# A split-fp32 FFN on one core: a product put off, the last two units reordered, the hidden output stored as ready-made blocks

## The chip, the cores and the metric

The kernel runs on one core of one Trainium2 chip. The metric is the device time of one execution in microseconds (us), lower is better. Engines are named as in the profile: PE (TensorE), DVE (VectorE), ACT (ScalarE), POOL (GpSimd), SP (the queue that issues the DMAs).

## What is computed

Four layers on x of 1024 tokens by 1024 features in float32: two hybrid layers, then two layers of retention and differential attention, each of which ends in an FFN. Only that FFN is touched:

```
u = rmsnorm_2(h, ffn_norm[l])
h = h + (jax.nn.silu(u @ w_gate[l]) * (u @ w_up[l])) @ w_down[l]   # hidden width 2816
```

## The kernel before

**Arithmetic.** A float32 product is made of three matmuls in a rounded format: high by high, high by low, low by high. So each operand is first split: ACT rounds it to `hi` (for weights L1268, L204, L1516; for activations L1202), and another engine subtracts, `lo = src - hi` (weights on POOL, L193 and L1517; activations on POOL or DVE, L1203). `block` (L1187 to 1196) issues the three matmuls for each 128-row chunk of the contraction (L1192, L1194, L1195).

**Seven products.** Both FFN products are cut 2 by 2 and made from seven block products in place of eight. The activations then stand as the blocks B11, B21, B22 and the differences T1 to T4; the weights get four DVE operations a unit (`combine`, L1321 to 1324 and L1500 to 1503), in place, so that w6, w3 take the place of the first row's two blocks and w7, w4 that of the second's.

**First half, `ffn_hidden` (L1272 to 1388).** 22 units: unit i makes 256 columns of the gate (i even) or the up projection (i odd) for all tokens; two units make a pair j. `first` runs two block products (24 matmuls), `second` the other five (60). Each of the four quadrants of a unit's result goes to `leave`. For the gate it is scaled by the row factor R (DVE, L230), ACT takes a tanh (L1285), DVE combines (L1286), and POOL multiplies by R again (L1287). For the up projection DVE multiplies it into the gate's z (L1281). After an odd unit the pair's two chunks of z go to DRAM (L1351). The FFN's normalized input lives as blocks in nine `xp` buffers and five in `fx`.

**Second half, `ffn_out` (L1461 to 1591).** The hidden chunks are taken in five groups of four (NSG) and two left over (`dense_ops`). A group has four units, one for each pair of output chunks, of 7 block products by 2 chunks by 3 matmuls, 42 in all. Seven DVE additions a unit take the products out of PSUM into the residual (L1561 to 1582); several of them must be done before PE may go on accumulating in the same bank. `hidden_blocks` (L1390) prepares the next group meanwhile: a list of steps, of which `some()` takes one at four places of each unit. A group's steps are: eight loads of 256 KB (L1401), eight DVE subtractions that make T1 to T4 (`minus`, L1417), and 14 splits (L1202, L1203). For group 0 the loads and the first steps stand in the last turn of the first half's loop, the rest ahead of the second half's first unit. A unit's weights are split in seven pieces of 256 columns (L1516, L1517).

**Order.** The program is built with `schedule_with_timeline_sim=True`: the order on each engine is set by a simulated timeline, so instructions that are independent do not run in the order in which they are written; `issue_after` adds an edge of order on one engine. A tile is a buffer of a pool (`xp` has 13, `wp` three for each of whi and wlo); whoever wants one that is in use waits until its last reader is done.

Of the kernel before, what the change touches and what calls it, by code (L numbers as in the profile page):

```python
# [24 lines left out]
P = 128  # L25
# [12 lines left out]
FDENSE = NH - 4 * NSG  # L38
LEAD, SW = 4, 2
IB, IT = 1, 2  # L40
EPS = 1e-6
# [31 lines left out]
class Builder:  # L73
    def __init__(self, nc, tc, a, es):
        self.nc, self.tc, self.a, self.es = nc, tc, a, es
        self.n = 0
        self.pools = {}
        self.chains = []
        self.ready, self.use_ready = [], False
        self.open(es, cp=1, rp=1, wp=3, xp=13, dp=6, sp=8)  # L80
        self.open(es, bass.MemoryType.PSUM, pa=3, ps=2, pt=2, po=1)
        self.open(es, bass.MemoryType.DRAM, dr=2)
# [1024 lines left out]
    def second(self, l, last):  # L1107
# [3 lines left out]
        with contextlib.ExitStack() as es:  # L1111
# [32 lines left out]
            self.open(es, fx=6, sw=SW, p1=LEAD)  # L1144
# [127 lines left out]
    def ffn_hidden(self, wg, wu, X, scale, more):  # L1272

        nc = self.nc
        Z, sums, hd = {}, {}, []

        def leave(i, u, t, src):
# [20 lines left out]
        def first(i, r, hold=False):  # L1298
            w = (wg, wu)[i % 2][i // 2 * 2]
            part = lambda j: (self.load_w(w[:, 4 * j:4 * j + 4, :]) if r is None else  # L1300
                              self.wsplit(r[:, 0, j * HW:(j + 1) * HW]))
# [25 lines left out]
        def second(i, w5, w3, w6, w7, w4):  # L1327
            s = sums.pop(i)
            C, E, B = self.psT(), self.psO(), self.psS()
            p5, w, u2, u3 = (self.d2() for _ in range(4))  # L1330
            self.block(C, self.wsplit(w5), X["T1"], True)
            nc.scalar.copy(p5, C)
            self.block(E, self.wsplit(w3), X["B22"], True)
            tt(w, E, p5, ALU.add)
            self.block(B, self.wsplit(w6), X["T2"], True)
            tt(u2, B, s, ALU.add)
            tt(w, w, u2, ALU.add)
            leave(i, 0, t1, w)
            self.block(B, self.wsplit(w7), X["T3"], False)
# [4 lines left out]
            self.block(C, self.wsplit(w4), X["T4"], True)  # L1344
            tt(u3, u3, C, ALU.subtract)
            leave(i, 1, t0, u3)
            if i % 2:
                z = Z.pop(i // 2)
                for u in range(2):
                    h = self.tl("dr", (P, S), tag="h", bufs=NH)  # L1350
                    nc.sync.dma_start(h, z[:, u, :])  # L1351
                    hd.append(h)

# [21 lines left out]
        for i in range(NH):  # L1375
            if i > 1:
                r = raw(i)
                if i == NH - 1:
                    ahead = self.hidden_blocks(hd, 0)
                    ahead[1].pop(0)()  # L1380
                if i >= LEAD:
                    first(i, r)
                ws.append(combine(r))
            if i == NH - 1:
                for _ in range(NAH):
                    ahead[1].pop(0)()
            second(i, *ws[i])
        return hd, ahead

    def hidden_blocks(self, hd, g):  # L1390
# [5 lines left out]
        def load(k):  # L1396
            two = self.tl("xp", (P, 4, HW))
            for h in range(2):
                for u in range(2):
                    f[u, h, k] = two[:, 2 * u + h, :]  # L1400
                    nc.sync.dma_start(f[u, h, k], hd[4 * g + 2 * u + k][:, h * HW:(h + 1) * HW])  # L1401

        def loads():
            for k in range(2):
                load(k)

        def put(name, k, slot, h, src, eng, sub=None):
            def step():
                if sub is not None:
                    sub()  # L1410
                if slot not in q:
                    q[slot] = self.tl("hx" if g % 2 else "xp", (P, 2, S), F32R)
                self.put_block(X, name, k, q[slot], h, f[src], eng)
            steps.append(step)

        def minus(eng, o, x, y):
            return lambda: eng.tensor_tensor(f[o], f[x], f[y], ALU.subtract)  # L1417

        for k in range(2):
            b11, b12, b21, b22 = (0, 0, k), (0, 1, k), (1, 0, k), (1, 1, k)  # L1420
            put("B11", k, k, 0, b11, v)
        for k in range(2):
            b11, b12, b21, b22 = (0, 0, k), (0, 1, k), (1, 0, k), (1, 1, k)
            put("T1", k, 2 + k, 0, b11, v, minus(v, b11, b12, b11))
        for k in range(2):
            put("B21", k, k, 1, (1, 0, k), p)
        for k in range(2):
            b11, b12, b21, b22 = (0, 0, k), (0, 1, k), (1, 0, k), (1, 1, k)
            put("B22", k, 2 + k, 1, b22, p, minus(v, b12, b22, b12))
            put("T2", k, 4 + k, 0, b22, v, minus(v, b22, b22, b11))  # L1430
        for k in range(2):
            b11, b12, b21, b22 = (0, 0, k), (0, 1, k), (1, 0, k), (1, 1, k)
            put("T3", k, 4 + k, 1, b12, p)
            put("T4", k, 6, k, b21, p, minus(v, b21, b21, b22))
        return X, [loads] + steps

    def dense_ops(self, wd, hd, c0):
# [5 lines left out]
        def load():  # L1443
            for c in range(c0, NH):
                o = self.tl("hx", (P, 2, S), F32R)
                f = self.tl("xp", (P, S))
                nc.sync.dma_start(f, hd[c])
# [30 lines left out]
    def ffn_out(self, l, hd, last, ahead):  # L1478
# [27 lines left out]
        parts, pmark = [], [None]  # L1506

        def wsplit(src):

            if not parts:  # L1510
                hi = self.tl("wp", (P, 4, P), F32R, tag="whi")
                lo = self.tl("wp", (P, 4, P), F32R, tag="wlo")
                parts.extend([(hi[:, 0:2, :], lo[:, 0:2, :]), (hi[:, 2:4, :], lo[:, 2:4, :])])
            hi, lo = parts.pop(0)
# [3 lines left out]
            return hi, lo  # L1518

        def weights(r):  # L1520
            w1, w2 = wsplit(r[0][:, 0:n]), wsplit(r[0][:, n:2 * n])
            return w1, w2, combine(r)
# [16 lines left out]
        X, steps = ahead  # L1539
        for f in steps:  # L1540
            f()
        residual(0)
        rs = raw(1)
        for i in range(4 * NSG):
# [12 lines left out]
            w1, w2, (w5, w3, w6, w7, w4) = ready  # L1557
# [4 lines left out]
            self.block(C, wsplit(w5), X["T1"], True)  # L1562
# [4 lines left out]
            self.block(A, wsplit(w6), X["T2"], False)  # L1567
# [4 lines left out]
            self.block(C, wsplit(w3), X["B22"], False)  # L1572
# [5 lines left out]
            w4 = wsplit(w4)  # L1578
# [159 lines left out]
def layout(i):  # L1738
# [22 lines left out]
    a["w_down_2"] = units(i["w_down_2"], KC)  # L1761
# [26 lines left out]
```

## Time and profile before

| | |
|---|---|
| three runs, median (lowest to highest) | 3586.26 us (3582.91 to 3586.89) |
| profiled execution, own time | 3588.15 us |
| its span, mean granted TensorE clock | 3586.4 us, 0.977 |
| first half of the FFN, steady part | 1660 to 2025 us, and 2905 to 3295 us in the other layer |
| from the first to the second half | 2025 to 2105 us, 3295 to 3365 us |
| second half, steady part | 2105 to 2290 us, 3365 to 3540 us |

A row of the windows view tells, for a stretch of the span, how long each engine was busy in it and with how many instructions, the clock that TensorE was granted, the share of the time in which the DMA engines were busy, and the rate. A row of the waits view tells who waited for whose result: us in total, how often, the longest. A wait in PE's column is time in which the array stands; idle time of another engine costs nothing by itself.

### The profile page before, as it was taken

The numbers are of one execution on the slowest core, as the hardware profiler recorded it, in microseconds if no ns is written. First come the engines' busy times: TensorE is split into PE (matmuls) and PEld (weight loads), VectorE is DVE, ScalarE is ACT, GpSimd is POOL, SyncE is SP. The second block draws the span as 40 slices with busy tenths as digits, with TensorE's granted clock in tenths as the row PEclk, the third lists the DMA queues.
The fourth block names the chain that finished last, engine by engine and source line by source line (L and its number), as shares of the span: only waits on it lengthen the run. The fifth ranks groups of instructions, "written<-read, shape, count | busy, mean of one in ns | idle before, by whom it ended". The sixth has DMA issues, their size and how long they took to land.

```text
span 3586.4 us, 46309 instructions
## 1 busy us (share of the span) xinstructions
PE 3390.6 (95%) x15948; PEld 2785.1 (78%) x15948; DVE 2508.4 (70%) x3963; ACT 1570.2 (44%) x3187; POOL 2088.5 (58%) x1859
## 2 busy tenths in 40 slices
PE   8999999899999999889999989999998899999897
PEld 6788888788888888767777767788887677777676
DVE  6756656755646766686777798766656767667997
ACT  4475442674444554352333333445543523333343
POOL 4785454884573344465666788733334556657884
PEclk9999999999999999999999999999998999999998
DMA  4112532112432223442112243311123422112432
GB/s 130 38 56 54 171 122 75 35 59 75 166 110 87 90 89 123 142 138 83 71 71 74 81 153 106 107 55 52 54 95 132 140 83 71 71 71 83 153 103 80
DMA packets 168956, 336.16 MB, mean 94 GB/s; under 512 B 32432, under 2 KB 43152, under 8 KB 168720
## 3 DMA queue, kind: packets, MB, share of 16 engines
q1 hardware_dynamic: 168720, 333.19, 28.3%
q8 instruction: 126, 2.06, 0.2%
q14 instruction: 110, 0.90, 0.1%
HBM read 253.90 MB, written 76.07 MB: 92 GB/s over the span
## 4 chain that ended last, share of the span: by engine, by line
PE 70%; DVE 13%; POOL 8%; issue 4%; ACT 2%; DMA 2%; SPq 0%; DVEq 0%; POOLq 0%; ACTq 0%
PE pa L221 11%; PE pa L223 11%; PE pa L224 11%; PE pa L1195 3%; PE pa L1192 3%; PE pa L1194 3%; PE po L426 3%; POOL wlo L193 3%; PE T L1195 3%; PE T L1192 2%; PE T L1194 2%; POOL cc L700 2%; PE T L415 2%; PE ps L333 2%; PE ps L334 2%
## 5 line engine op out<-in xcount | busy, mean ns | idle before, releaser
L221 PE MATMUL pa<-xp,whi 128*128 128x512 f32 x2048 | 814.3, 399 | 21.1 <-ACT xp L188 11.9
L223 PE MATMUL pa<-xp,whi 128*128 128x512 f32 x2048 | 815.0, 398 | 6.8 <-DVE xp L189 6.7
L224 PE MATMUL pa<-xp,wlo 128*128 128x512 f32 x2048 | 814.4, 398 | 0.2 <-POOL wlo L193 0.2
L193 POOL TENSOR_TENSOR wlo<-raw,whi 128x512 fp32r<-128x512 f32 x304 | 427.5, 1406 | 480.6 <-ACT whi L204 468.6
L193 POOL TENSOR_TENSOR wlo<-xp,whi 128x512 fp32r<-128x512 f32 x248 | 358.7, 1449 | 193.2 <-ACT whi L1268 192.2
L221 PEld LDWEIGHTS pa<-xp,whi 128*128 128x128 f32 x2048 | 390.1, 191 | 98.3 <-ACT xp L188 12.0
L223 PEld LDWEIGHTS pa<-xp,whi 128*128 128x128 f32 x2048 | 389.9, 190 | 86.0 <-DVE xp L189 10.9
L224 PEld LDWEIGHTS pa<-xp,wlo 128*128 128x128 f32 x2048 | 390.1, 190 | 76.5 <-POOL wlo L193 0.6
L1268 ACT CAST whi<-xp 128x512 fp32r<-128x512 f32 x248 | 153.9, 620 | 409.1 <-PE pa L1194 136.6
L204 ACT CAST whi<-raw 128x512 fp32r<-128x512 f32 x304 | 187.2, 616 | 280.8 <-PE pa L223 171.7
L1192 PE MATMUL pa<-xp,whi 128*128 128x512 f32 x672 | 270.3, 402 | 36.1 <-DVE xp L1576 9.0
L445 POOL TENSOR_SCALAR p<-p,st 128x256 f32<-128x256 f32 (+4 forms) x224 | 156.3, 706 | 225.2 <-DVE st L1038 116.4
L1195 PE MATMUL pa<-xp,wlo 128*128 128x512 f32 x672 | 266.2, 399 | 3.0 <-POOL wlo L193 3.0
L1194 PE MATMUL pa<-xp,whi 128*128 128x512 f32 x672 | 266.4, 396 | 0.0
L700 POOL TENSOR_TENSOR cc<-cc,prod 128x256 f32<-128x256 f32 x240 | 201.0, 858 | 30.0 <-ACT prod L699 23.8
L1192 PEld LDWEIGHTS pa<-xp,whi 128*128 128x128 f32 x672 | 128.7, 191 | 76.3 <-ACT whi L1516 15.9
L419 DVE TENSOR_TENSOR tp<-T,tp 128x512 fp32r<-128x512 f32 (+2 forms) x224 | 131.7, 598 | 68.3 <-ACT tp L418 67.6
L426 PE MATMUL po<-tp,xp 128*128 128x256 f32 (+1 forms) x1024 | 163.1, 279 | 5.9 <-ACT tp L418 5.4
L426 PEld LDWEIGHTS po<-tp,xp 128*128 128x128 f32 x1024 | 148.7, 189 | 24.6 <-ACT tp L418 9.2
L699 ACT ACTIVATE prod<-cc,c 128x256 f32<-128x256 f32 x240 | 119.0, 507 | 109.0 <-POOL cc L700 97.6
L1033 ACT ACTIVATE p<-p,st 128x384 f32<-128x384 f32 (+3 forms) x192 | 117.1, 611 | 108.9 <-DVE st L1026 107.0
L1287 POOL TENSOR_TENSOR xp<-xp,R 128x512 f32<-128x512 f32 x80 | 111.3, 1391 | 86.0 <-DVE xp L1286 86.0
(324 smaller groups left out, 8149.1 us busy)
## 6 DMA issues: line engine op xcount, KB each, us to landing
raw<-w_in SPq DMA_DIRECT2D x208, 256.0 KB, 2.8
xp<-x SPq DMA_DIRECT2D x48, 512.0 KB, 7.4
xp<-w_gate SPq DMA_DIRECT2D x44, 512.0 KB, 4.9
xp<-w_up SPq DMA_DIRECT2D x44, 512.0 KB, 5.3
raw<-w_out SPq DMA_DIRECT2D x80, 256.0 KB, 2.9
x<-xp SPq DMA_DIRECT2D x80, 256.0 KB, 2.0
h<-xp SPq DMA_DIRECT2D x40, 512.0 KB, 2.9
xp<-h SPq DMA_DIRECT2D x80, 256.0 KB, 4.3
```

The costliest lines, as they stand in the source:

```text
L193: self.last_rest = self.nc.gpsimd.tensor_tensor(lo, src, hi.bitcast(F32), ALU.subtract)
L204: nc.scalar.copy(hi, raw)
L221: nc.tensor.matmul(ps[h], hi[:, k - k0, :], x[:, 0, t], start=(k == 0), stop=False)
L223: nc.tensor.matmul(ps[h], hi[:, k - k0, :], x[:, 1, t], start=False, stop=False)
L224: nc.tensor.matmul(ps[h], lo[:, k - k0, :], x[:, 0, t], start=False, stop=(k == nk - 1))
L426: nc.tensor.matmul(O[:, qs[0] * P:qs[0] * P + w], lhsT, pt[part][:, o:o + w], start=((kt, qs) == blocks[0] and i == 0), stop=((kt, qs) == ...
L445: self.nc.gpsimd.tensor_scalar(out, src, colm, 1.0, ALU.mult, ALU.mult)
L700: nc.gpsimd.tensor_tensor(acc[:, i:i + CPW], acc[:, i:i + CPW], q, ALU.add)
L1192: nc.tensor.matmul(ps, hi[:, k, :], xh, start=(start and k == 0), stop=False, skip_group_check=True)
L1194: nc.tensor.matmul(ps, hi[:, k, :], xl, start=False, stop=False, skip_group_check=True)
L1195: nc.tensor.matmul(ps, lo[:, k, :], xh, start=False, stop=(k == len(ops) - 1), skip_group_check=True)
L1268: self.nc.scalar.copy(hi, src)
```

## The change

It touches the FFN of both layers, in three places, and gives `wp` a fourth buffer for each of its tags (the weights' hi and lo everywhere in the kernel).

1. In `leave` the multiplication by R on POOL is queued in a list, and issued behind four more weight splits (AGE), or when the up projection's quadrant needs it.
2. In the loop over units, `first` of the last unit (21) comes ahead of `second` of the one before, and the loads ahead for group 0 come after it.
3. A pair's z is stored as seven blocks, B11, T1, B21, B22, T2, T3, T4 in this order; the four differences are made here, by four DVE subtractions into a buffer `tq`. `hidden_blocks` loads them in four DMAs a group, two blocks each (the last one: one), and only splits. The two chunks that are left over are stored as before. To pair the chunks in this new way the rows of `w_down` are permuted in `layout`.

Beside that `ffn_out` splits a unit's weights in three pieces of 512 columns and one of 256, and loads the first residual ahead of group 0's steps.

```diff
-        self.open(es, cp=1, rp=1, wp=3, xp=13, dp=6, sp=8)
+        self.open(es, cp=1, rp=1, wp=4, xp=13, dp=6, sp=8)
...
-            self.open(es, fx=6, sw=SW, p1=LEAD)
+            self.open(es, fx=6, sw=SW, p1=LEAD, tq=1)
...
             if i % 2:
+                flush((i - 1, u, t.start))
                 nc.vector.scalar_tensor_tensor(z, src, 0.5, z, ALU.mult, ALU.mult)
                 return
...
-            nc.gpsimd.tensor_tensor(z, z, self.R[:, t], ALU.mult)
+            late.append((cnt[0], (i, u, t.start), lambda: nc.gpsimd.tensor_tensor(
+                z, z, self.R[:, t], ALU.mult)))
+
+        def flush(until=None):
+            while late and (until in [k for _, k, _ in late] if until else
+                            late[0][0] + AGE <= cnt[0]):
+                with self.tc.issue_after(self.last_rest.ins):
+                    late.pop(0)[2]()
+
+        def wsplit(src):
+            out = self.wsplit(src)
+            cnt[0] += 1
+            flush()
+            return out
...
+            if j % 2 == 0:
+                hd.append(self.tl("dr", (P, len(BLOCKS), 2, HW), tag="hb", bufs=NSG))
+            d = hd[-1][:, :, j % 2, :]
+            nc.sync.dma_start(d[:, 0, :], z[:, 0, t0])
+            nc.sync.dma_start(d[:, 2:4, :], z[:, 1, :].rearrange("p (b t) -> p b t", b=2))
+            t = self.tl("tq", (P, 4, HW))
+            tt(t[:, 0, :], z[:, 0, t1], z[:, 0, t0], ALU.subtract)
+            tt(t[:, 1, :], z[:, 1, t1], t[:, 0, :], ALU.subtract)
+            tt(t[:, 2, :], z[:, 1, t1], z[:, 0, t1], ALU.subtract)
+            tt(t[:, 3, :], z[:, 1, t0], t[:, 1, :], ALU.subtract)
+            nc.sync.dma_start(d[:, 1, :], t[:, 0, :])
+            nc.sync.dma_start(d[:, 4:7, :], t[:, 1:4, :])
...
         for i in range(NH):
-            if i > 1:
+            if i > 1 and i < NH - 1:
                 r = raw(i)
-                if i == NH - 1:
-                    ahead = self.hidden_blocks(hd, 0)
-                    ahead[1].pop(0)()
                 if i >= LEAD:
                     first(i, r)
                 ws.append(combine(r))
+            if i == NH - 2:
+                r = raw(NH - 1)
+                first(NH - 1, r)
             if i == NH - 1:
+                ahead = self.hidden_blocks(hd, 0)
+                ahead[1].pop(0)()
+                ws.append(combine(r))
                 for _ in range(NAH):
                     ahead[1].pop(0)()
             second(i, *ws[i])
...
+        def load(i):
+            n = min(2, len(BLOCKS) - i)
+            two = self.tl("xp", (P, 2, 2, HW))
+            nc.sync.dma_start(two[:, 0:n], hd[g][:, i:i + n])
...
+        steps.append(lambda: (load(0), load(2)))
...
-            put("T1", k, 2 + k, 0, b11, v, minus(v, b11, b12, b11))
+            put("T1", k, 2 + k, 0, v)
+        steps.append(lambda: load(4))
...
         ready = weights(raw(0))
         X, steps = ahead
+        residual(0)
         for f in steps:
             f()
-        residual(0)
...
-            self.block(A, wsplit(w6), X["T2"], False)
+            w6, w3 = wsplit(r[0])
+            self.block(A, w6, X["T2"], False)
...
-            self.block(A, wsplit(w7), X["T3"], False)
+            w7, w4 = wsplit(r[1])
+            self.block(A, w7, X["T3"], False)
```

## Rows read from the trace of the kernel before

**Rows 1.** The page, part 1: busy us, share, instructions.

```profile
PE 3390.6 (95%) x15948; PEld 2785.1 (78%) x15948; DVE 2508.4 (70%) x3963; ACT 1570.2 (44%) x3187; POOL 2088.5 (58%) x1859
```

**Rows 2.** Windows, six stretches: us, then PE, PEld, DVE, ACT, POOL, clock, DMA, GB/s.

```profile
1660.00:2025.00 365.00, 348.81 (x1500) 279.93 (x1499) 255.21 (x282) 116.48 (x197) 228.31 (x160) 1.00 0.21 77
2025.00:2105.00 80.00, 66.20 (x266) 50.52 (x265) 76.66 (x94) 31.87 (x67) 65.76 (x52) 0.94 0.43 152
2105.00:2290.00 185.00, 171.89 (x718) 133.97 (x717) 161.89 (x234) 74.28 (x174) 146.69 (x148) 0.99 0.31 95
2905.00:3295.00 390.00, 372.57 (x1588) 298.35 (x1588) 273.17 (x305) 122.25 (x207) 242.57 (x172) 0.99 0.23 81
3295.00:3365.00 70.00, 56.60 (x219) 42.83 (x218) 67.68 (x83) 28.15 (x63) 57.00 (x48) 0.90 0.43 151
3365.00:3540.00 175.00, 162.40 (x684) 126.64 (x684) 155.13 (x225) 68.94 (x164) 140.53 (x143) 1.00 0.29 88
```

**Rows 3.** Waits of PE, whole span: us in total, times, longest.

```profile
PE T L1195 <- POOL wlo L193: 33.6, 20, 2.0
...
PE T L1192 <- DVE xp L1563: 10.8, 8, 1.6
PE pa L1192 <- DVE xp L1561: 9.1, 6, 3.1
PE pa L1192 <- DVE xp L1576: 9.0, 8, 1.8
PE ps L1192 <- DVE dp L1336: 8.7, 4, 3.7
...
PE T L1192 <- ACT hx L1202: 3.1, 4, 1.4
```

**Rows 4.** Timeline of POOL near 1790 us: start, us, instruction, [idle before it].

```profile
1789.83 1.68 POOL L1287 TENSOR_TENSOR xp<-xp,R 128x512 f32<-128x512 f32 x1 [1.96 <-DVE xp L1286]
1791.47 1.71 POOL L193 TENSOR_TENSOR wlo<-sw,whi 128x512 fp32r<-128x512 f32 x1
```

**Rows 5.** Timeline of ACT there.

```profile
1788.46 0.62 ACT L1268 CAST whi<-sw 128x512 fp32r<-128x512 f32 x1 [1.08 <-PE ps L1194]
```

**Rows 6.** Waits of POOL, 1660 to 2040 us.

```profile
POOL xp L1287 <- DVE xp L1286: 38.7, 36, 2.0
```

**Rows 7.** Waits of ACT, 1660 to 2040 us.

```profile
ACT whi L1268 <- PE ps L1194: 72.3, 37, 2.5
```

**Rows 8.** Waits of DVE, 1660 to 2040 us.

```profile
DVE xp L230 <- PE pa L1195: 31.9, 9, 3.5
```

**Rows 9.** L1417, whole span, then 2040 to 2105 us: ns min/median/max.

```profile
L1417 DVE TENSOR_TENSOR xp<-xp x80: 671/934/1786, 2042.9 to 3499.3; 128x512 f32<-128x512 f32 x80
...
L1417 DVE TENSOR_TENSOR xp<-xp x15: 674/1183/1769, 2042.9 to 2104.8; 128x512 f32<-128x512 f32 x15
```

**Rows 10.** The weight splits on POOL, L193 and L1517: ns min/median/max.

```profile
L193 POOL TENSOR_TENSOR wlo<-xp,whi x248: 1282/1297/1851, 1621.0 to 3310.7; 128x512 fp32r<-128x512 f32 x124
...
L1517 POOL TENSOR_TENSOR wlo<-raw,whi x120: 717/744/1282, 2055.8 to 3527.0; 128x256 fp32r<-128x256 f32 x120
```

**Rows 11.** Groups by form, 2040 to 2105 us: POOL's activation splits of group 0.

```profile
L1203 POOL TENSOR_TENSOR xp<-xp,xp 128x512 fp32r<-128x512 f32 x8 | 13.4, 1694 | 0.8 <-ACT xp L1202 0.8
```

**Rows 12.** Timeline of SP, 2005 to 2110 us: the loads of group 0.

```profile
2022.58 7.64 SPq L1401 DMA_DIRECT2D xp<-h  x8
```

**Rows 13.** The page, part 6: KB each, median us to landing.

```profile
xp<-w_gate SPq DMA_DIRECT2D x44, 512.0 KB, 4.9
...
h<-xp SPq DMA_DIRECT2D x40, 512.0 KB, 2.9
xp<-h SPq DMA_DIRECT2D x80, 256.0 KB, 4.3
```

**Rows 14.** Windows, two short stretches of the transitions (columns as in rows 2).

```profile
2050.00:2075.00 25.00, 16.76 (x56) 12.05 (x57) 24.37 (x29) 8.55 (x19) 20.86 (x17) 0.80 0.53 193
...
3320.00:3340.00 20.00, 16.59 (x65) 12.87 (x64) 18.31 (x28) 7.40 (x18) 12.94 (x14) 0.91 0.90 340
```

More of the change, by code (lines that the diff above doesn't have):

```diff
@@ L38 @@
 FDENSE = NH - 4 * NSG
+BLOCKS = ["B11", "T1", "B21", "B22", "T2", "T3", "T4"]
 LEAD, SW = 4, 2
 IB, IT = 1, 2
+AGE = 4
 EPS = 1e-6
@@ L1275, in ffn_hidden @@
         Z, sums, hd = {}, {}, []
+        late, cnt = [], [0]
         def leave(i, u, t, src):
@@ L1338, in second @@
             leave(i, 0, t1, w)
-            self.block(B, self.wsplit(w7), X["T3"], False)
+            self.block(B, wsplit(w7), X["T3"], False)
             tt(u3, B, s, ALU.add)
@@ L1343, in second @@
             C = self.psT()
-            self.block(C, self.wsplit(w4), X["T4"], True)
+            self.block(C, wsplit(w4), X["T4"], True)
             tt(u3, u3, C, ALU.subtract)
@@ L1394, in hidden_blocks @@
         v, p = nc.vector, nc.gpsimd
[L1396 to L1407, printed above, removed]
+        def load(i):
+            n = min(2, len(BLOCKS) - i)
+            two = self.tl("xp", (P, 2, 2, HW))
+            nc.sync.dma_start(two[:, 0:n], hd[g][:, i:i + n])
+            for j in range(n):
+                for k in range(2):
+                    f[BLOCKS[i + j], k] = two[:, j, k, :]
@@ L1408, in step, with put @@
+        def put(name, k, slot, h, eng):
             def step():
-                if sub is not None:
-                    sub()
                 if slot not in q:
                     q[slot] = self.tl("hx" if g % 2 else "xp", (P, 2, S), F32R)
-                self.put_block(X, name, k, q[slot], h, f[src], eng)
+                self.put_block(X, name, k, q[slot], h, f[name, k], eng)
             steps.append(step)
-        def minus(eng, o, x, y):
-            return lambda: eng.tensor_tensor(f[o], f[x], f[y], ALU.subtract)
+        steps.append(lambda: (load(0), load(2)))
@@ L1427, in hidden_blocks @@
         for k in range(2):
-            b11, b12, b21, b22 = (0, 0, k), (0, 1, k), (1, 0, k), (1, 1, k)
-            put("B22", k, 2 + k, 1, b22, p, minus(v, b12, b22, b12))
-            put("T2", k, 4 + k, 0, b22, v, minus(v, b22, b22, b11))
+            put("B22", k, 2 + k, 1, p)
+            put("T2", k, 4 + k, 0, v)
+        steps.append(lambda: load(6))
         for k in range(2):
-            b11, b12, b21, b22 = (0, 0, k), (0, 1, k), (1, 0, k), (1, 1, k)
-            put("T3", k, 4 + k, 1, b12, p)
@@ L1434, in hidden_blocks @@
-            put("T4", k, 6, k, b21, p, minus(v, b21, b21, b22))
-        return X, [loads] + steps
+            put("T3", k, 4 + k, 1, p)
+            put("T4", k, 6, k, p)
+        return X, steps
     def dense_ops(self, wd, hd, c0):
@@ L1504, in combine @@
             return s1, a12, a11, a21, a22
-        parts, pmark = [], [None]
+        pmark = [None]
         def wsplit(src):
[L1510 to L1514, printed above, removed]
+            m = src.shape[1] // P
+            hi = self.tl("wp", (P, 4, P), F32R, tag="whi")[:, 0:m, :]
+            lo = self.tl("wp", (P, 4, P), F32R, tag="wlo")[:, 0:m, :]
             src = src.rearrange("p (k e) -> p k e", e=P)
@@ L1517, in wsplit @@
             pmark[0] = nc.gpsimd.tensor_tensor(lo, src, hi.bitcast(F32), ALU.subtract)
-            return hi, lo
+            return [(hi[:, k:k + 2, :], lo[:, k:k + 2, :]) for k in range(0, m, 2)]
         def weights(r):
-            w1, w2 = wsplit(r[0][:, 0:n]), wsplit(r[0][:, n:2 * n])
-            return w1, w2, combine(r)
+            return wsplit(r[0]), combine(r), r
         def residual(p):
@@ L1556, in ffn_out @@
                     ops, w, prep[:] = self.dense_ops(wd, hd, 4 * NSG)
-            w1, w2, (w5, w3, w6, w7, w4) = ready
+            (w1, w2), (w5, _, _, _, _), r = ready
             x0, x1 = xs[2 * p], xs[2 * p + 1]
@@ L1760, in layout @@
     a["w_up_2"] = units(i["w_up_2"], NH)
-    a["w_down_2"] = units(i["w_down_2"], KC)
+    wd = units(i["w_down_2"], KC)
+    order = [4 * g + c for g in range(NSG) for c in (0, 2, 1, 3)] + list(range(4 * NSG, NH))
+    a["w_down_2"] = wd[:, :, :, order, :]
     z = np.zeros(RPB_PAD, np.float32)
```

28 lines of the change are left out of this document (14 added, 14 removed).

## The prediction

> **What bounds the kernel now.** Start with the page's first part: PE is busy 95% of the span [rows 1], so a change can only win by filling holes in PE, and the question is where they are. The windows view, cut at the stages of the FFN, answers it [rows 2]: subtract PE's busy time from the length. In the first half PE stands 365.0 - 348.8 = 16.2 us and, in the other layer, 390.0 - 372.6 = 17.4; in the transitions 13.8 and 13.4; in the second half 13.1 and 12.6. That is 86.5 us in all, the most that the change can win from holes. In the transitions the granted clock is besides 0.94 and 0.90 of full (2.4 GHz), so part of the matmuls there ran at the lower level (1.2 GHz); about 66.2 x 0.06 + 56.6 x 0.10 = 9.6 us more lie there, my estimate.
>
> PE's waits name the holes [rows 3]. The first half has one: 20 waits, 33.6 us, ten in each layer, for the low part of a weight split on POOL. That is all of its 16.2 + 17.4 us. The other rows are of DVE: L1336 and the additions L1561, L1563, L1576 that must leave PSUM before PE may go on, and ACT's split of a group's first block.
>
> How POOL comes to be late is seen in one instance [rows 4, 5]. ACT has rounded w5 at 1788.46 + 0.62 = 1789.1. POOL could subtract then, but its next instruction is the product by R, which stood 1.96 us for DVE's L1286, began at 1789.83 and took 1.68; the split began at 1791.47, 2.4 us late. One such wait for each pair of units fits: only a gate unit (even) ends in that product. POOL stands 38.7 us in this stage for DVE in that way, in 36 waits [rows 6].
>
> In the transition DVE is the full engine: 76.7 of 80 us, POOL 65.8 [rows 2]. In the second half DVE is busy 161.9 of 185 us (88%), in the first only 255.2 of 365 (70%). So one subtraction costs something in the later stages that it need not cost in the first.
>
> **The change, part by part.**
>
> *The product put off.* The same 88 products run on POOL, behind four more splits. Removed: up to the 33.6 us [rows 3]. The late work then is one 2.4 us hole less, and what waits on the product is only the up unit's multiplication a unit later. The fourth `wp` buffer helps too: ACT now waits for PE to give back a weight buffer, 72.3 us on one row alone [rows 7], so splits can run a block further ahead. Elsewhere I cost that buffer at nothing: in the whole span PE's waits for L193 are the 33.6 us and some smaller ones.
>
> *The subtractions moved into the first half.* Per layer 40 leave the second half, and 4 come in for each of ten pairs, 80 in all on either side. Their duration there: median 0.93 us, 0.67 at least and 1.79 at most [rows 9]; so 3.7 us a pair, 2.7 to 7.1. A pair is 168 matmuls; the stretch with 1500 holds 8.9 pairs, and DVE is idle 365 - 255.2 = 109.8 us in it, 12.3 a pair. Queued behind them on DVE are the next gate unit's first scaling and the next weight combinations, and behind these ACT and POOL. The cover is plain: before L230, DVE stands 3.5 us for PE, nine times [rows 8], which is just when a pair has ended. DVE goes from 70 to (255.2 + 8.9 x 3.7) / 365 = 79% or so. Bounds for what PE then loses: nothing (as now at 70%), or every subtraction in full, 20 x 3.7 = 74 us. The nearest row is the second half, where at 88% PE loses 13.1 us in 185 with seven additions on its path per 42 matmuls; here the path has about one (u2, before T3) in 84, so an eighth as often per matmul. An eighth of 13.1 x 365 / 185 is 3.2 us a layer. I take 3 each, 6 in all. First half: -33.6 + 6 = -27.6.
>
> *The transition.* Of group 0's preparation the eight subtractions go; DVE did them at a median of 1.18 us [rows 9], on a full engine: 9.4 us a layer, 18.9 in all. Bounds: little, if POOL is next (it has eight splits of 1.69 us for that group, 13.5 us [rows 11], unchanged, plus weight splits), say 4 a layer; or the whole hole with its clock, 13.8 + 4.0. I take 18.9. Running unit 21's `first` earlier frees four `xp` buffers one `second` (60 matmuls, 14 us) sooner, so the first steps of group 0 can run beside PE's work; that makes the sum safer, and I add nothing for it. Moving the loads behind that `first` costs nothing visible: they were issued from 2022.58 [rows 12], and pair 1, which they need, is stored long before.
>
> *The second half.* The other 32 subtractions a layer go, about 25 of them in the steady part: 25 x 0.93 = 23 us less for DVE, (161.9 - 23) / 185 = 75%, near the first half's level at which PE does not wait for DVE. Weight splits: seven of 0.74 to 1.28 us become three of 1.30 to 1.85 and one of the former [rows 10], 5.2 by the shortest against 4.6, so POOL saves some and crosses DVE less. Of the holes, 13.1 + 12.6, I take half, 12.9 us; the other half I leave to the waits that stay. Bounds: 0 to 25.7.
>
> *DMA.* Stores grow by the three blocks more of a pair, 0.75 MB, in 39 us of first half: hidden behind a stage that uses the DMA engines a fifth of its time. Loads: a group takes 3.5 MB in four issues where it took 2 MB in eight. At the 340 GB/s that the busiest stretch shows [rows 14] the 1.5 MB more are 4.6 us, and I take a 1 MB load to land later than the 512 KB one, which takes 4.9 [rows 13]. ACT would meet that at a group's first split, where PE now loses 3.1 us in four waits [rows 3]; I double it, +3.
>
> **Sum.** -27.6 - 18.9 - 12.9 + 3 = -56.4. The profiled execution took 3588.15, 1.9 above the median of the three runs; taken from the median the forecast is 3586.3 - 56 = **3530 us**.
>
> **The rivals.**
>
> *1. POOL is late all the same.* The four subtractions have two inputs in SBUF, as POOL's operations have, and the two slow each other: the same POOL split takes 1.28 us or up to 1.85 [rows 10], the same subtraction 0.67 to 1.79 [rows 9]. Four of them at a pair's end push POOL by up to 4 x 0.57 = 2.3 us, as much as the 2.4 us now saved, at the very place of the wait. Then the first half gains nothing: -18.9 - 12.9 + 3 = -29, 3557 us. For it: the place. Against: the split now has a buffer more of lead, and rows 7 show ACT ready long before. The Trainium skill (SBUF — State Buffer, "Who interferes with whom") says that VectorE with two SBUF inputs and GpSimd share a port pair as an exclusive lock, and that the second to come fully blocks until the first ends. The longest rows are somewhat shorter than that (1.79 is less than 0.67 + 1.28), so the trace bears it out as a delay, not as a whole wait each time.
>
> *2. The later stages gain nothing*, because POOL's splits bound the transition (82% busy now) and the larger loads the groups' starts: -27.6 + 3 to 4, 3562 us. For it: POOL's 65.8 of 80 us. Against: DVE's rows, not POOL's, stand in PE's waits.
>
> *3. Slower: DVE becomes the bound of the first half.* Place: the end of each pair, where four subtractions stand ahead of what PSUM waits for. Price: a pair costs them in full, 20 x 3.7 = 74 us, and the old holes stay: +74 - 29 = +45, 3631 us. It decides once DVE's work for a pair, now 255.2 / 8.9 = 28.7 us, reaches PE's 39: with four at the longest 1.79 it is 35.8, so it needs a bad order as well as the longest times.
>
> *4. No change*: the planner orders the engines by its own times, and puts the product or the subtractions where they hold up as much as they relieve: 3586 us.
>
> **How the numbers follow.** Forecast 0.60; rival 1 0.15; rival 2 0.11; rival 3 0.08; no change 0.06. A change of under 0.2% (7 us) can't be told from none in a measurement of this kernel. So faster 0.60 + 0.15 + 0.11 = 0.86, same 0.06, slower 0.08. The forecast's own bounds: about 22 us better (transition's clock and half of the rest of the second half), about 20 worse. With rivals 1 and 2 the range is 3508 to 3572; left out are rivals 3 and 4 and a small tail below.
>
> **What would show it.** Right: in the first half no wait of PE for L193, POOL's wait for L1286 near nothing, DVE near 80% and PE's idle time below 5 us a layer; in the transitions no L1417, PE idle about 4 to 5 us, a clock above 0.95; in the second half DVE near 75% and PE idle 6 to 7. Wrong: PE waits of the first half that name DVE (L1336, L1340) or again L193 with DVE's new line just before; ACT standing for the loads of blocks; or a first half as long as before.

## The result, and the profile after

Four runs of the changed kernel have a median of 3546.52 us (3544.79 to 3548.47), those of the kernel before beside them 3585.21: a ratio of 0.9893, interval 0.9876 to 0.9910, some 39 us faster. The forecast was 3530, in the range 3508 to 3572. The time lies in the range, some 16 us above the forecast: 39 us came of the 56 that were forecast, and most of the terms behind them did not come as priced.

Where the time went is best read from four events of each layer's FFN that both kernels have: the first copy of a sum by ACT (the first half begins), the last subtraction of the first unit, that of the last unit, and the last addition of the second half. The source view gives their first and last start; in layer 0, before (L1305, L1345, L1582):

```profile
L1305 ACT COPY p<-pa x22: 573/579/582, 1588.2 to 2036.9; 128x512 f32<-128x512 f32 x22
...
L1345 DVE TENSOR_TENSOR dp<-dp,T x22: 673/674/680, 1644.2 to 2068.4; 128x512 f32<-128x512 f32 x22
...
L1582 DVE TENSOR_TENSOR xp<-pa,xp x20: 672/679/692, 2084.1 to 2293.7; 128x512 f32<-128x512 f32 x20
```

and after (L1323, L1363, L1610):

```profile
L1323 ACT COPY p<-pa x22: 575/580/589, 1588.3 to 2020.4; 128x512 f32<-128x512 f32 x22
...
L1363 DVE TENSOR_TENSOR dp<-dp,T x22: 672/675/682, 1633.7 to 2057.9; 128x512 f32<-128x512 f32 x22
...
L1610 DVE TENSOR_TENSOR xp<-pa,xp x20: 673/681/692, 2080.8 to 2272.0; 128x512 f32<-128x512 f32 x20
```

So "start" is 1644.2 - 1588.2 = 56.0 us and now 45.4; "steady" 2068.4 - 1644.2 = 424.2 and now 424.2; "second" (transition and second half) 225.3 and now 214.1. All kernels of this study, both layers (L0 / L1), read in the same way:

| kernel | start | steady | second | median of the runs, us |
|---|---|---|---|---|
| before | 56.0 / 55.3 | 424.2 / 423.9 | 225.3 / 224.8 | 3585.21 |
| after | 45.4 / 47.2 | 424.2 / 419.0 | 214.1 / 215.3 | 3546.52 |
| b_wp4 | 46.5 / 47.4 | 402.7 / 401.2 | 224.9 / 225.2 | 3530.30 |
| b_late | 55.4 / 54.0 | 423.9 / 423.8 | 225.6 / 224.9 | 3584.36 |
| b_wp4_late | 44.9 / 49.4 | 402.7 / 402.1 | 222.2 / 223.6 | 3530.76 |
| b_wp4_reorder | 47.0 / 44.8 | 414.6 / 411.4 | 223.6 / 224.3 | 3552.33 |
| b_wp4_split | 45.8 / 47.6 | 399.3 / 399.8 | 227.6 / 227.9 | 3530.19 |
| b_wp4_subs | 46.2 / 44.8 | 411.9 / 414.0 | 223.7 / 224.7 | 3551.13 |
| b_blocks | 48.2 / 47.1 | 420.4 / 419.3 | 215.5 / 213.4 | 3541.95 |
| b_blocks_nosub | 46.6 / 46.8 | 416.3 / 410.8 | 209.9 / 210.4 | 3518.39 |
| a_loads | 44.9 / 47.1 | 421.3 / 417.3 | 215.4 / 215.8 | 3542.17 |
| a_wp3 | 55.6 / 55.4 | 444.2 / 446.4 | 223.1 / 221.3 | 3622.84 |
| c_deep | 48.7 / 49.0 | 418.3 / 417.3 | 212.8 / 212.8 | 3542.95 |
| c_spread | 44.8 / 46.9 | 426.2 / 425.4 | 219.9 / 217.3 | 3556.63 |

The change won 18.7 us in the two starts, for which nothing was forecast, 4.9 in the steady parts, for which 27.6 were, and 20.7 in the transitions and second halves, for which 28.8 were. Of these 44.3 us, 2.8 were lost outside the three columns: the profiled spans differ by 41.5.

The "steady" column is not pairs of units alone, since its end is the last unit, beside which group 0 is prepared. A pair, read from the starts of the same subtraction two units apart in the middle of the stage, typically takes 40.9 us before, 41.0 after and in b_blocks, and about 39 in b_wp4. The last unit takes 30.5 us before, 30.0 in b_wp4, and 24.8 in b_blocks, where group 0's subtractions are gone (layer 0).

PE's waits of the changed kernel, whole span; the first row answers to the first of [rows 3], L196 being L193 of before:

```profile
PE T L1198 <- POOL wlo L196: 28.7, 17, 2.1
...
PE pa L1195 <- ACT whi L1544: 9.7, 4, 4.5
...
PE pa L1195 <- ACT whi L1271: 9.3, 4, 3.1
...
PE pa L1195 <- DVE xp L1605: 5.7, 9, 1.2
PE pa L1195 <- DVE xp L1588: 4.4, 8, 0.7
...
PE T L1195 <- DVE xp L1590: 1.7, 6, 0.3
```

PE still waits for the low split that the put-off was to bring in time, 28.7 us where it was 33.6. The timeline of POOL near one of them, and PE's own row:

```profile
1704.09 2.99 POOL L1292 TENSOR_TENSOR xp<-xp,R 128x512 f32<-128x512 f32 x2
1707.03 3.76 POOL L196 TENSOR_TENSOR wlo<-xp,whi 128x512 fp32r<-128x512 f32 x3
```

```profile
1708.35 0.50 PE L1198 MATMUL T<-xp,wlo 128*128 128x512 f32 x1 [1.73 <-POOL wlo L196]
```

Two products stand in a row, 2.99 us, ahead of the split whose end, 1707.03 + 1.3, PE waits 1.73 us for. So the wait has moved. In [rows 4] it was for the split of w5 (`wlo<-sw`), behind one product; here that product comes behind w5's split, a little later in the same timeline:

```profile
1733.40 1.67 POOL L196 TENSOR_TENSOR wlo<-sw,whi 128x512 fp32r<-128x512 f32 x1 [1.36 <-ACT whi L1271]
1735.03 1.74 POOL L1292 TENSOR_TENSOR xp<-xp,R 128x512 f32<-128x512 f32 x1
```

### The profile page after: what moved, and what is told of

The parts are those of the page before. It is cut to its first block, busy times and chain, and to the rows that moved or that the text cites. A ratio compares the mean times of both kernels' runs of the same rounds, so it can differ in the third digit from the quotient of the medians.

```text
span 3544.9 us, 45991 instructions
## 1 busy us (share of the span) xinstructions
PE 3380.3 (95%) x15948; PEld 2780.8 (78%) x15948; DVE 2524.3 (71%) x3963; ACT 1545.9 (44%) x3067; POOL 2048.3 (58%) x1739
## 4 chain that ended last, share of the span: by engine, by line
PE 61%; DVE 15%; POOL 10%; DMA 6%; issue 5%; ACT 2%; SPq 0%; POOLq 0%; DVEq 0%; ACTq 0%
PE pa L224 11%; PE pa L226 11%; PE pa L227 11%; DMA xp<-w_up 3%; PE po L429 3%; POOL wlo L196 3%; PE pa L1195 3%; PE pa L1198 3%; PE pa L1197 3%; POOL cc L703 2%; PE T L418 2%; PE ps L336 2%; PE ps L337 2%; PE T L1198 2%; PE T L1195 1%
## 5 line engine op out<-in xcount | busy, mean ns | idle before, releaser
L224 PE MATMUL pa<-xp,whi 128*128 128x512 f32 x2048 | 813.8, 398 | 21.2 <-ACT xp L191 10.9
L196 POOL TENSOR_TENSOR wlo<-raw,whi 128x512 fp32r<-128x512 f32 x304 | 425.5, 1400 | 482.5 <-ACT whi L207 468.0
L196 POOL TENSOR_TENSOR wlo<-xp,whi 128x512 fp32r<-128x512 f32 x248 | 366.1, 1491 | 197.4 <-ACT whi L1271 192.4
L227 PEld LDWEIGHTS pa<-xp,wlo 128*128 128x128 f32 x2048 | 389.7, 190 | 75.4 <-issue 0.5
L1198 PEld LDWEIGHTS pa<-xp,wlo 128*128 128x128 f32 x672 | 129.6, 193 | 42.2 <-POOL wlo L196 13.9
```

The lines of the kernel that those rows point to most:

```text
L196: self.last_rest = self.nc.gpsimd.tensor_tensor(lo, src, hi.bitcast(F32), ALU.subtract)
L224: nc.tensor.matmul(ps[h], hi[:, k - k0, :], x[:, 0, t], start=(k == 0), stop=False)
L227: nc.tensor.matmul(ps[h], lo[:, k - k0, :], x[:, 0, t], start=False, stop=(k == nk - 1))
L1198: nc.tensor.matmul(ps, lo[:, k, :], xh, start=False, stop=(k == len(ops) - 1), skip_group_check=True)
```

## The experiments

Twelve kernels were run, each beside the kernel before on the same chip. The names: b_ starts from the kernel before, a_ from the changed one, c_ looks for a better one.

**The buffer alone (b_wp4).**

```diff
-        self.open(es, cp=1, rp=1, wp=3, xp=13, dp=6, sp=8)
+        self.open(es, cp=1, rp=1, wp=4, xp=13, dp=6, sp=8)
```

> The kernel before with a fourth buffer for the weights' hi and lo, and nothing else. Theory A: the fourth buffer is what shortened the start of the first half (from the first copy of a sum to unit 0's last subtraction, 56.0 and 55.3 us before, 45.4 and 47.2 after), since ACT can split the leading units' weights while PE stands for the row scale; then the start becomes 46 to 48 us, the steady part and the second half stay, and the time falls by 15 to 19 us. Rival B: the product put off did it, as POOL no longer stands for DVE there; then nothing changes (within 4 us).

Measured: 3530.30 us, ratio 0.9845 (0.9829 to 0.9862), 55 us. The start is as theory A has it. But the steady part also falls by 21.5 and 22.7 us, which no theory named. (Starts and steady parts make 61.6 us together; 6.5 are lost behind the last additions of the two layers.) The windows of layer 0's steady part, before and here, columns as in [rows 2]:

```profile
1644.20:2068.40 424.20, 397.27 (x1676) 316.08 (x1674) 308.94 (x337) 137.62 (x235) 272.92 (x189) 0.98 0.22 80
```

```profile
1634.60:2037.30 402.70, 392.66 (x1686) 317.70 (x1684) 316.67 (x337) 134.17 (x234) 276.82 (x189) 0.99 0.24 85
```

PE's idle time falls from 26.9 to 10.0 us; the other 4.6 us are its busy time. PE's waits (1640 to 2030 us) and one of ACT's rows (1660 to 2000 us, where it was 64.4 before; the 72.3 of [rows 7] are of a little longer stretch):

```profile
PE ps L1192 <- DVE dp L1336: 5.4, 1, 5.4
PE po L1192 <- DVE dp L1334: 3.3, 1, 3.3
PE T L1195 <- POOL wlo L193: 0.5, 2, 0.3
```

```profile
ACT whi L1268 <- PE ps L1194: 17.1, 16, 2.2
```

All rows of that kind together, ACT's L1268 waiting for the L1194 of one or the other accumulator, fall from 195.1 to 70.9 us in this stretch: ACT stands much less for weight buffers that PE still reads. The windows view of 200 us in the middle: PE has next to no hole left. (The two waits for DVE come at the end of the stage, behind 2000 us.)

```profile
1700.00:1900.00 200.00, 199.68 (x865) 161.97 (x865) 149.16 (x165) 65.81 (x114) 136.16 (x96) 1.00 0.22 79
```

The edit also changed the planner's order. Though the product is written as before, it now runs behind the split of w5, not ahead of it as in [rows 4]:

```profile
1765.89 1.84 POOL L193 TENSOR_TENSOR wlo<-sw,whi 128x512 fp32r<-128x512 f32 x1 [0.47 <-ACT whi L1268]
1770.87 1.57 POOL L193 TENSOR_TENSOR wlo<-xp,whi 128x512 fp32r<-128x512 f32 x1 [3.14 <-PE ps L1195]
1772.40 1.74 POOL L1287 TENSOR_TENSOR xp<-xp,R 128x512 f32<-128x512 f32 x1
```

POOL's wait for L1286 is 15.1 us here, in 18 times, and was 35.6 in 32 (1660 to 2000 us). So the run shows what the edit is worth. How much of it is the free buffer itself and how much the other order that it allowed, no run separates.

**The product put off alone (b_late).**

```diff
-            nc.gpsimd.tensor_tensor(z, z, self.R[:, t], ALU.mult)
+            late.append((cnt[0], (i, u, t.start), lambda: nc.gpsimd.tensor_tensor(
+                z, z, self.R[:, t], ALU.mult)))
...
```

> The kernel before with the product by R put off behind four splits, and nothing else. Theory A: the put-off alone takes POOL's wait of 1.7 us a pair away, and the changed kernel lost that again to weight loads that stand behind the new stores; then the steady part (424.2 and 423.9 us) falls by 12 to 16 us a layer, the time by 24 to 32. Rival B: the products now stand in pairs ahead of the same split, and the put-off moves the wait without removing it; then the steady part falls by less than 4 us a layer, and PE's waits for the low split stay at 20 to 34 us in all. Rival C on the start: it falls to 46 to 48 us here.

Measured: 3584.36 us, ratio 0.9996 (0.9986 to 1.0005). Nothing. The timeline of POOL at the place of [rows 4] tells why:

```profile
1785.10 1.68 POOL L1290 TENSOR_TENSOR xp<-xp,R 128x512 f32<-128x512 f32 x1 [1.96 <-DVE xp L1289]
1786.73 1.72 POOL L194 TENSOR_TENSOR wlo<-sw,whi 128x512 fp32r<-128x512 f32 x1
```

The same order, the same 1.96 us for DVE, the same 1.68. The planner runs instructions in the order of its simulated timeline, not as written; there this product is still ahead of that split. PE's row is unchanged too: 33.5 us in 20 waits, and the starts are not those of rival C. The figures are rival B's, but not for its reason: the put-off moved nothing, the order is that of before. What the product would be worth if it did run later is not shown by this run. With the fourth buffer (b_wp4_late) the put-off is again worth nothing:

```diff
-        self.open(es, cp=1, rp=1, wp=3, xp=13, dp=6, sp=8)
+        self.open(es, cp=1, rp=1, wp=4, xp=13, dp=6, sp=8)
...
+            late.append((cnt[0], (i, u, t.start), lambda: nc.gpsimd.tensor_tensor(
+                z, z, self.R[:, t], ALU.mult)))
...
```

> The kernel before with the fourth buffer and the product put off. Theory A: with the buffer PE has nothing left to wait for in the steady part (402.7 and 401.2 us), so the put-off changes nothing; the steady part stays at 399 to 405 us and the time at 3526 to 3535. Rival B: products in pairs ahead of a split bring waits back; then the steady part gets longer by 5 us a layer or more.

Measured: 3530.76, theory A.

**The named parts without the buffer (a_wp3).** Against the changed kernel:

```diff
-        self.open(es, cp=1, rp=1, wp=4, xp=13, dp=6, sp=8)
+        self.open(es, cp=1, rp=1, wp=3, xp=13, dp=6, sp=8)
```

> The changed kernel with three weight buffers in place of four: all named parts of the change, without the buffer. Theory A: the buffer is the gain, the rest costs the first half what it gives the second; then the start is 54 to 56 us again, the steady part 430 us or more, the second half 214 to 220, and the time 3575 to 3600 us. Rival B: the named parts gain by themselves and the buffer only comes on top; then the time is 3565 us or less.

Measured: 3622.84 us, ratio 1.0105 (1.0090 to 1.0120), slower than before by 37. The first half is as A says, the steady part 20 and 22.5 us longer; the second half, 223.1 and 221.3, gains less than was expected, and the time lies above A's 3575 to 3600. PE's waits, whole span:

```profile
PE T L1198 <- POOL wlo L196: 52.6, 20, 3.1
```

20 waits as before, but 2.6 us each where they were 1.7.

**The last two units alone (b_wp4_reorder).** On top of the buffer:

```diff
-            if i > 1:
+            if i > 1 and i < NH - 1:
...
+            if i == NH - 2:
+                r = raw(NH - 1)
+                first(NH - 1, r)
             if i == NH - 1:
+                ahead = self.hidden_blocks(hd, 0)
+                ahead[1].pop(0)()
+                ws.append(combine(r))
```

> The kernel before with the fourth buffer and the new order of the last two units, with loads ahead for group 0 after unit 21's first products. Theory A: unit 21's weights are loaded later than before and PE stands for them, 3 to 5 us and some clock, against a transition that starts better prepared; then steady part and second half together (627.6 and 626.4 us) change by less than 4 us either way. Rival B: the transition gains what was forecast, 5 us a layer or more, since buffers are free sooner. Rival C: the late load costs 5 us a layer or more.

Measured: 3552.33, 22 us over b_wp4, and rival C. The chain of waits tells it (start, us, what):

```profile
1985.65 0.70 DVE xp L1281
...
1986.37 0.33 SPq L1351
...
1986.80 4.96 DMA xp<-w_up
...
1991.84 0.63 ACT whi L1268
```

The store of pair 9 stands on SP's queue for that pair's last product; the load of unit 21's weights is behind it, as it was before. Only now `first` of unit 21 needs them a whole `second` sooner. PE stands 5.7 us for ACT's rounding of them (waits of PE, 1950 to 2010 us):

```profile
PE pa L1192 <- ACT whi L1268: 5.7, 1, 5.7
```

The granted clock follows the holes. In the windows view the stretch with this one, and one in the transition where PE is busy half the time, read 0.93 and 0.72 (in b_wp4 the stretch from 1950 to 2000 us reads 1.00):

```profile
1950.00:2000.00 50.00, 43.58 (x176) 34.38 (x176) 34.06 (x38) 14.32 (x25) 28.46 (x20) 0.93 0.32 116
...
2025.00:2050.00 25.00, 13.06 (x42) 9.12 (x42) 20.97 (x25) 7.30 (x14) 17.33 (x13) 0.72 0.41 149
```

**Stored blocks, without the other two parts (b_blocks).** The changed kernel with the product at once and the old order of the units:

```diff
-            late.append((cnt[0], (i, u, t.start), lambda: nc.gpsimd.tensor_tensor(
-                z, z, self.R[:, t], ALU.mult)))
+            nc.gpsimd.tensor_tensor(z, z, self.R[:, t], ALU.mult)
...
-            if i == NH - 2:
-                r = raw(NH - 1)
-                first(NH - 1, r)
...
```

> The kernel before with the fourth buffer, the stored blocks and the larger weight pieces of the second half; the product at once and the old order of the last two units. Theory A: the second half (225.3 and 224.8 us before, 214.1 and 215.3 after) gets its whole gain from this part, 19 to 22 us in both layers together, and the steady first half gets longer than before, by 4 to 10 us a layer, since weight loads stand behind the stores on SP's queue. Rival B: the stores cost the first half nothing, and its steady part stays within 3 us; then what the put-off promised was never there. Rival C: the second half owes its gain to the order of the last two units; then it stays at 220 us or more here.

Measured: 3541.95 us, 12 over b_wp4. The second half has all of its gain, as theory A says. The steady part is 4 us shorter than in the kernel before, which no theory had; that is its last unit, 5.7 us shorter, while a pair takes as long as before. Against b_wp4, the right thing to compare with, since both have the buffer, it is 17.7 and 18.1 us longer, and 23 without the last unit. PE's waits in it (1632 to 2052 us) have the old row back, about once a pair:

```profile
PE T L1198 <- POOL wlo L196: 15.2, 9, 2.1
```

**The price of the subtractions, and of the stores.** b_wp4_subs adds to b_wp4:

```diff
+                if i // 2 < 2 * NSG:
+                    t = self.tl("tq", (P, 4, HW))
+                    tt(t[:, 0, :], z[:, 0, t1], z[:, 0, t0], ALU.subtract)
...
```

> The kernel before with the fourth buffer, and after each of the first ten pairs the four subtractions on DVE into a buffer that nobody reads; no other part of the change (the added work isn't used). The price of the subtractions alone. Theory A: they are what costs the steady first half 18 us a layer where blocks are stored (402.7 and 401.2 us with the buffer alone, 420.4 and 419.3 with the blocks), because DVE then gives the combined weights to ACT and POOL later; then the steady part is 414 to 422 us here, and PE waits for the low split again, about once a pair. Rival B: the stores and the longer life of the pair's buffer cost it; then the steady part stays at 400 to 406 us.

b_blocks_nosub leaves them out of b_blocks and stores copies in their place, so it computes another result and only its time counts:

```diff
-            t = self.tl("tq", (P, 4, HW))
-            tt(t[:, 0, :], z[:, 0, t1], z[:, 0, t0], ALU.subtract)
...
-            nc.sync.dma_start(d[:, 1, :], t[:, 0, :])
-            nc.sync.dma_start(d[:, 4:7, :], t[:, 1:4, :])
+            nc.sync.dma_start(d[:, 1, :], z[:, 0, t1])
+            nc.sync.dma_start(d[:, 4, :], z[:, 0, t1])
+            nc.sync.dma_start(d[:, 5:7, :], z[:, 1, :].rearrange("p (b t) -> p b t", b=2))
```

> The kernel with the fourth buffer and the stored blocks, where the four subtractions of a pair are left out: T1 to T4 are stored as copies of z's quadrants, so the second half multiplies other numbers, in the same time. Theory A (the subtractions cost the steady part): it is 401 to 406 us, the second half stays at 213 to 216, and the time is about 3508 us. Rival B (the stores): the steady part stays at 415 to 421 us.

Neither theory holds alone. The subtractions by themselves cost the steady part 9.2 and 12.8 us, 21 in the runs (3551.13). Without them the stored blocks still cost it 13.6 and 9.6, or 18.1 and 13.8 without the last unit, which they shorten; both together cost 18, or 23. The second half of b_blocks_nosub is also 5.6 and 3.0 us shorter than that of b_blocks, which no run explains. In the kernel with the subtractions alone, PE is no longer full (windows, then PE's wait, 1640 to 2046 us):

```profile
1700.00:1900.00 200.00, 196.20 (x848) 158.48 (x847) 159.02 (x183) 64.63 (x113) 132.41 (x92) 1.00 0.22 79
```

```profile
PE T L1195 <- POOL wlo L193: 6.2, 8, 1.3
```

DVE is at 80% there (159.0 of 200) against 75% in b_wp4.

**Did the weight loads stand behind the stores (a_loads)?** The four subtractions and the stores written behind the next `raw`:

```diff
-            if i % 2:
-                leave_blocks(i // 2, Z.pop(i // 2))
...
                 r = raw(i)
+                if i == NH - 2:
+                    r_last = raw(NH - 1)
+                leave_pair(i)
```

> The changed kernel with the stores of a pair, and its four subtractions, written behind the load of the next unit's weights (for the last pair stored, behind the loads of units 20 and 21). Theory A: the weight loads stood behind the stores on SP's queue, DVE 21.5 and 12.4 us for them in the steady part, and unit 21's load cost PE 4 us and the clock; with the loads ahead DVE's waits for weight loads fall below 5 us a layer, the steady part falls by 6 to 12 us a layer, and the time by 12 to 22 us against the changed kernel. Rival B: the loads were late but nobody who mattered waited; then the time stays within 4 us. Rival C: the buffers of the pair are held longer, the next loads wait for those, and it gets slower by 5 us or more.

Measured: 3542.17, ratio 0.9882 (0.9867 to 0.9896); the interval overlaps that of the changed kernel, as rival B has it. But the run does not decide between the theories. In the steady part the loads did not move on SP's queue; the rows of the changed kernel, then of this one:

```profile
1722.79 0.37 SPq L1381 DMA_DIRECT2D hb<-xp  x1
1723.26 0.41 SPq L1310 DMA_DIRECT2D xp<-w_up  x1
```

```profile
1723.23 0.37 SPq L1379 DMA_DIRECT2D hb<-xp  x1
1723.71 0.41 SPq L1310 DMA_DIRECT2D xp<-w_up  x1
```

The load still follows the pair's stores, and DVE's wait for these loads (1660 to 2000 us) is 18.3 us against 21.5 in the changed kernel, where A wanted less than 5. Only unit 21's load moved, from 2007 to 1978 us. What speaks for rival B is b_wp4: DVE waits 21.0 us for them there too, and PE has next to no hole.

**Larger weight pieces alone (b_wp4_split).** On top of the buffer:

```diff
-            self.block(A, wsplit(w6), X["T2"], False)
+            w6, w3 = wsplit(r[0])
+            self.block(A, w6, X["T2"], False)
...
-            self.block(A, wsplit(w7), X["T3"], False)
+            w7, w4 = wsplit(r[1])
+            self.block(A, w7, X["T3"], False)
```

> The kernel before with the fourth buffer and the larger weight pieces of the second half (three of 512 columns and one of 256 a unit in place of seven of 256), subtractions in the second half as before. Theory A: the second half gained because the subtractions left it; then it stays at 222 to 226 us with the larger pieces alone. Rival B: fewer and larger splits on POOL gave the gain, since POOL then slows DVE less; then it falls to 213 to 217 us, and the time to about 3510.

Measured: 3530.19; the second half 227.6 and 227.9, a little longer than theory A's 222 to 226. The larger pieces gain nothing there; the gain came with the stored blocks.

**Two tries at a better one.** c_spread issues the subtractions one at a time in the next pair, with z of every other pair in `fx`; c_deep adds one more pair of weight buffers. Both start from b_blocks:

```diff
+            m = tt(w, E, p5, ALU.add)
+            one(m)
...
-                Z[i // 2] = self.tl("xp" if i else "fx", (P, 2, S))
+                Z[i // 2] = self.tl("xp" if i // 2 % 2 else "fx", (P, 2, S))
```

```diff
-            self.open(es, fx=6, sw=SW, p1=LEAD, tq=1)
+            self.open(es, fx=6, sw=SW, p1=LEAD, tq=1, wq=1)
...
+        pool = "wp" if self.nsplit % 5 else "wq"
+        self.nsplit += 1
+        hi = self.tl(pool, (P, m, P), F32R, tag="whi")
```

> The kernel with the fourth buffer and the stored blocks, with a pair's four subtractions issued one at a time during the next pair, each behind an addition of the second five products, and z of every other pair in the free fx buffer. Theory A: the four in a row at the pair's end delay the weight combination; spread out they fit into DVE's idle time (25% of the steady part), the steady part falls from 420 to 402 to 408 us, the second half keeps its 214, and the time is 3510 to 3520 us. Rival B: it is DVE's load and not the place; then the steady part stays at 414 us or more.

> The kernel with the fourth buffer and the stored blocks, with a fifth pair of weight buffers in the first half of the FFN (all that the memory holds). Theory A: what the subtractions and stores cost the steady part is lead time of the weight splits, which one more buffer gives back as the fourth one did; then the steady part falls from 420 to 402 to 410 us, the second half keeps 213 to 216, and the time is 3510 to 3525 us, less than any so far. Rival B: the combined weights come late from DVE itself, so a free buffer can't be filled sooner; then the steady part stays at 416 us or more.

c_spread: 3556.63, worse than b_blocks in both halves; its steady part is as rival B has it (414 or more), and why it grew is not shown. c_deep: 3542.95, as b_blocks, with rival B's steady part (416 or more). The buffer does remove waits of the steady part (PE's waits, 1632 to 2052 us, where b_blocks has 15.2):

```profile
PE T L1199 <- POOL wlo L196: 2.6, 5, 0.9
```

but PE then stands for the second half's first weights (1990 to 2080 us), and the steady part, 418.3 us in layer 0, is hardly shorter than the 420.4 of b_blocks:

```profile
PE pa L1196 <- ACT whi L1542: 5.6, 1, 5.6
PE T L1196 <- ACT whi L1542: 5.5, 1, 5.5
```

So the best kernel of the study that computes the FFN is the one before with the buffer alone: 3530 us, 16 less than the changed one. (b_wp4_late and b_wp4_split, which add to it, are as fast.)

## Why the prediction came out, and what in it was wrong

**The time came into the range by luck.** The first half was to gain 27.6 us in its steady parts and nothing in its starts; it gained 4.9 and 18.7. A sign of being wrong that the prediction named came true: a steady first half as long as before (424.2 us in layer 0, before and after). That the forecast total, 56 us, is what the buffer alone gives (55) is chance; the buffer had no price of its own in the sum. All the other parts together cost 16 us on top of it, and 37 without it.

**The product put off (-33.6).** This is the step that failed. What was read was right: POOL was late by the product, ten times a layer. What was concluded, that writing the product later takes it away, was tested by b_late and is wrong: the planner's order at the place did not change. The order that it was to bring, the product behind the split of w5, comes with the fourth buffer, put-off or not: in the steady part of layer 0 it is there pair after pair in b_wp4, b_wp4_late, b_blocks and the changed kernel, and not in b_late and a_wp3. The sentence that the buffer "helps too" had cause and help reversed. [rows 7] had shown it: ACT stood 72.3 us on one row alone for weight buffers, so the splits had little lead, and POOL's delay reached PE. With a buffer more, and the order that the planner then makes, POOL still stands 15.1 us for DVE with the product at once (b_wp4), and PE waits for the low split 0.5 us.

**"Elsewhere I cost that buffer at nothing."** Wrong: b_wp4 gains 55 us by it, 17.4 of them in the two starts, and b_late, with 1.9 there, shows that the put-off does not bring them. How is less well shown: the leading units' weights can be split while PE stands for the row scale; in b_wp4 and the changed kernel the fourth sum is copied 1.0 us behind the third, in the kernel before 12.2 (L1305, layer 0). But c_deep has 13.8 us there and a start of 48.7, so that is not all of it. The prediction cut its stretches at 1660 us and never read that stage, in which PE stood 10.3 and 10.9 us; so its 86.5 us were not all the holes that there were to win.

**The subtractions (+6).** Mis-sized: 22 us in the two steady parts (b_wp4_subs), and not by PE waiting for additions, from which the 6 were worked out, but again for the low split on POOL. The working had a slip besides: one addition in 84 matmuls against seven in 42 is a fourteenth, not an eighth, so its own rows give 1.8 us a layer in place of 3.2, still further off. The rows of DVE's idle time were a total; that it was slack for the chain from the weight combination over ACT and POOL to PE was an assumption.

**The order of the last two units (0).** The prediction priced the loads of group 0 that were moved and left out the load that `first` of unit 21 waits for, which was not moved. 22 us with the buffer alone. In the changed kernel it is not seen as much: put-off and order together stand at 3546.5 against 3542.0 of b_blocks, and the intervals of the two ratios overlap.

**Transition and second half (-18.9 - 12.9 + 3).** The mechanism was right, the size 20.7 in place of 28.8. No subtraction is left there, and PE's waits for the additions L1588, L1590 and L1605 shrank to 4.4, 1.7 and 5.7 us, from 9.1, 10.8 and 9.0 [rows 3]. What took their place: 9.7 us for weights of the second half that ACT rounds (L1544), most of it in one wait of each layer's transition; before it was 5.0 (L1516). The +3 for larger loads did not come: PE has no wait for ACT's split of a block (L1205) in the changed kernel, where the kernel before had 3.1 us (L1202).

**The rivals.** Rival 1, POOL late all the same, came true in its row (28.7 us, 17 waits), not by its mechanism. In b_wp4_subs POOL's splits take 1485 ns in the mean and 1471 in b_wp4: the subtractions hardly slow them. The exclusive lock of the Trainium skill (SBUF — State Buffer, "Who interferes with whom") is seen in single durations of this case: in the kernel before, DVE's L1322 takes 1.73 us from 1783.18, just behind the start of a split of 1.29 on POOL at 1783.08, and 0.69 from 1788.45, when POOL stands: 1.04 us more, of the 1.19 that the split still had to run, nearer to a whole wait than the prediction read it. But there DVE is the one that waits, and 14 ns a split on POOL decide nothing. Rival 2, nothing in the later stages, is not so: 20.7 us came there. Rival 3, slower, is near in size to what the named parts do without the buffer: 3622.84, forecast 3631, but by waits for the split, not for additions. Rival 4's planner is what kept the put-off from working in b_late, though not the change as a whole.

**What stays open**: how the stores alone (b_blocks_nosub) cost the steady part 10 to 14 us. The pair's buffer lives longer and the planner's order is another; no run here separates these. The order is another in every run with a fourth buffer too, so that the lead of the splits is the cause of the 55 us is argued from ACT's waits, not shown by itself.

## What to carry to other kernels

Where an engine waits for buffers to come back and the one behind it is just in time, try one more buffer by itself before anything else; it costs one digit, and here it was worth more than everything in the change together. One more is not always worth something: with the stored blocks a fifth brought nothing (c_deep). Where a planner sets the order, text that is moved is not work that is moved (b_late on POOL, a_loads on SP): look at the engine's timeline afterwards, at the place where the wait was. A step that is pulled forward pulls its loads only if they are pulled forward too.

## What was not expected

That one buffer more, 128 by 512 hi and lo, closes nearly all of PE's holes in the pairs while every engine does the same work in another order. The starts of the sums' copies (L1305, layer 0) come 19.5 and 21.4 us apart by turns in the kernel before, and 19.0 to 19.7 in b_wp4, with PE busy 199.68 of 200 us at a granted clock of 1.00.
